# One PSUM bank for all attention outputs, scaled four heads at a time

## The chip, the cores and the metric

One core of one Trainium2 chip runs the whole layer. The metric is the device time of one execution, in microseconds (us), of which three runs of the kernel before gave 663.7, 664.32 and 665.25 us; the median is 664.32 us.

## The reference: what is computed

A decoder layer on 512 tokens of width 1024, in float32: an RMS norm, one input projection, two token mixers side by side (an mLSTM of 4 heads, and a sparse attention of 8 heads of width 64), an output projection, a gated MLP with a short convolution, and a last RMS norm. The change is in the attention. For each block of 128 queries an indexer scores all keys, the best 128 are kept, and the softmax runs over the kept keys only:

```python
logits = einsum('bqhd,bqkhd->bqhk', qa, ks) * (A_DH ** -0.5) + bias      # 8 heads, 4 blocks of 128 queries
p   = softmax(where(valid, logits, -inf), axis=-1)
out = einsum('bqhk,bqkhd->bqhd', p, vs)                                  # 64 outputs for each query and head
```

The kernel doesn't gather: it adds a large negative number to the logits of keys that were not kept, takes the exponentials, multiplies them with all values up to the block's last key, and divides by the row sum at the end. This last step is called the scaling here.

## The kernel before, in words

The order of the instructions on each engine is the order in which the program issues them. A stage has a main list of steps (the matmuls of a projection, in three products of split float32 parts) and side lists; `merge` spreads the side lists over the main list by their costs, at compile time. Each engine then works off its own queue in order and waits where an operand isn't ready.

The attention is the side list `att_steps` (L660 to L755). It has 32 items: item number 8t + h is head h of query block t, t from 0 to 3. It runs as a pipeline. Step i issues, in this order:

- the logits of item i on TensorE (L691, L692 and, for t < 3, L694), into one of three "lg" banks;
- the transposes of item i-3 (L702), copied to SBUF as `pT` by ScalarE (L707) or, for odd heads of block 3, by VectorE (L705);
- for item i-1 the addition of bias and logits with the row minimum on VectorE (L716, called the row reduction below), and the exponential with its row sum on ScalarE (L719);
- in even steps two subtractions on VectorE for later queries (`second`, L680, two instructions a step);
- for block 3 one addition on GpSimd (L727);
- for item i-5 the product of `pT` with the values (L734, called the value product below): t+1 matmuls, into 64 columns of the "av" bank. In the records each of these fp32 matmuls counts twice.

There is one "av" bank of 128x512. In the kernel before, each block takes it anew at head 0 (L731). After head 7 of a block, VectorE takes the reciprocals of the eight row sums (L738, 128x8) and scales the whole bank with one instruction (L741, 128x512). It writes into the place of the block's queries in `aqT`, which were read before. Head 7 of block t falls into step 8t+12, and head 0 of block t+1 into step 8t+13.

The attention runs beside the projections of the mLSTM's inputs (`to_conv` and `to_mv`, L884 to L888). VectorE also has the top-128 search of block 3 there (L533, L536), convolution taps (L778), gate sums (L587 to L591, L610, L612) and the decays of two heads (L815, L819). GpSimd has splits of weights (L125) and casts of queries (L672). The attention outputs are transposed in the next stage (`to_mix`).

Of the kernel before, what the change touches and what calls it, by code (L numbers as in the profile page):

```python
# [10 lines left out]
F32 = mybir.dt.float32  # L11
# [33 lines left out]
def hybrid_layer(ctx: ExitStack, tc: tile.TileContext, a, out):  # L45
    nc = tc.nc
# [5 lines left out]
    small = ctx.enter_context(tc.tile_pool(name="small", bufs=2))  # L52
# [7 lines left out]
    def bank(tag):  # L60
        return ps.tile([128, 512], F32, name="bank_" + tag, tag=tag, bufs={"mm": 2, "lg": 3, "tp": 2, "av": 1}[tag])
# [213 lines left out]
    aqT, av = qv[:, 0:4, :], qv[:, 4:8, :]  # L275
# [173 lines left out]
    def backwards(v):  # L449

        (p, _), (step, n) = v.ap
        return bass.AP(tensor=v.tensor, offset=v.offset + (n - 1) * step, ap=[[p, 128], [-step, n]])
# [199 lines left out]
    ha, rsum, pout = {}, {}, {}  # L652
# [3 lines left out]
    def zeros():  # L656
        nc.gpsimd.tensor_scalar(qlz.rearrange("p a b c -> p (a b) c"), ident[:, None, :].to_broadcast([128, 4, 128]), 0.0,
                                None, op0=OP.mult)

    def att_steps(ts):  # L660
        items = [(t, h) for t in ts for h in range(8)]
        n = len(items)
        lg, ll, lp, qp = {}, {}, {}, {}

        def queries(j):

            t, g = divmod(j, 2)
            qd = ap.tile([128, 2, 2, 128], F32R, name="qd", tag="Q", bufs=2)
            src = aqT[:, 2 * g:2 * g + 2, t * 128:(t + 1) * 128]
            for i, a_, b_ in ((0, slice(0, 64), slice(64, 128)), (1, slice(64, 128), slice(0, 64))):  # L670
                nc.scalar.activation(qd[a_, :, i, :], src[a_], AF.Copy)
                nc.gpsimd.tensor_copy(qd[b_, :, i, :], src[a_])  # L672
            qp[j] = qd

        def second(p):

            t, c = divmod(p, 4)
            src = aqT[:, c, t * 128:(t + 1) * 128]
            for i, a_ in ((0, slice(0, 64)), (1, slice(64, 128))):
                nc.vector.tensor_tensor(qlz[a_, p % 2, i, :], src[a_], qp[p // 2][a_, c % 2, i, :].bitcast(F32), OP.subtract)  # L680

        def step(i):
            if i % 4 == 1 and i // 4 + 1 < n // 4:
                queries(i // 4 + 1)
            if i < n:
                t, h = items[i]
                w = (t + 1) * 128
                lg[i] = bank("lg")
                w2 = max(w, 256)
                qd = qp[i // 4]  # L690
                nc.tensor.matmul(lg[i][:, :w2], qd[:, h // 2 % 2, h % 2, :], kS[:, h, :w2], start=True, stop=False)  # L691
                nc.tensor.matmul(lg[i][:, :w2], qlz[:, i // 2 % 2, h % 2, :], kS[:, h, :w2], start=False, stop=t >= 3)  # L692
                if t < 3:
                    nc.tensor.matmul(lg[i][:, :w2], identb, keep[t] if t else causal[:, None, :].to_broadcast([128, 2, 128]),  # L694
                                     start=False, stop=True)
            if 0 <= i - 3 < n:
                t, h = items[i - 3]
                w = (t + 1) * 128
                l = ll.pop(i - 3)
                pt = bank("tp")  # L700
                for j in range(t + 1):
                    nc.tensor.transpose(pt[:, j * 128:(j + 1) * 128], l[:, j * 128:(j + 1) * 128], ident)  # L702
                pT = ap.tile([128, 512], F32, name="pT", tag="wA", bufs=3)
                if t >= 3 and h % 2:
                    nc.vector.tensor_copy(pT[:, :w], pt[:, :w])  # L705
                else:
                    nc.scalar.activation(pT[:, :w], pt[:, :w], AF.Copy)  # L707
                lp[i - 3] = pT
            if 0 <= i - 1 < n:
                t, h = items[i - 1]  # L710
                w = (t + 1) * 128
                if h == 0:
                    rsum[t] = small.tile([128, 8], F32, name="rs")
                l = ap.tile([128, 512], F32, name="l", tag="wB", bufs=3)
                nm = small.tile([128, 1], F32, name="nm", bufs=4)
                nc.vector.tensor_tensor_reduce(l[:, :w], lg.pop(i - 1)[:, :w],  # L716
                                               backwards(bias["T"][:, h, :w]) if t < 3 else score[t], -1.0, 3.0e38,
                                               OP.add, OP.min, nm)
                nc.scalar.activation(l[:, :w], l[:, :w], AF.Exp, bias=nm, scale=-1.0,  # L719
                                     accum_out=rsum[t][:, h:h + 1])  # L720
                ll[i - 1] = l
            if i and i % 2 == 0 and i // 2 + 1 < n // 2:
                second(i // 2 + 1)
            if i < n and items[i][0] >= 3:

                t, h = items[i]
                nc.gpsimd.tensor_tensor(score[t], backwards(bias["T"][:, h, :(t + 1) * 128]), keep[t], OP.add)  # L727
            if 0 <= i - 5 < n:
                t, h = items[i - 5]
                if h == 0:  # L730
                    pout[t] = bank("av")  # L731
                pT, po = lp.pop(i - 5), pout[t]
                for j in range(t + 1):
                    nc.tensor.matmul(po[:, h * 64:(h + 1) * 64], pT[:, j * 128:(j + 1) * 128],  # L734
                                     av[:, j, h * 64:(h + 1) * 64], start=(j == 0), stop=(j == t))
                if h == 7:
                    rr = small.tile([128, 8], F32, name="rr")
                    nc.vector.reciprocal(rr, rsum[t])  # L738

                    ha[t] = aqT[:, :, t * 128:(t + 1) * 128]  # L740
                    nc.vector.tensor_tensor(ha[t].rearrange("p c (h d) -> p c h d", h=2),  # L741
                                            po.rearrange("p (c h d) -> p c h d", c=4, h=2),
                                            rr.rearrange("p (c h) -> p c h", c=4)[:, :, :, None].to_broadcast([128, 4, 2, 64]),
                                            OP.mult)
        def costed(i):
            def f():
                step(i)
            f.cost = items[min(i, n - 1)][0] + 2.947
            return f
        def ready():  # L750
            zeros()
            queries(0)
            second(0)
            second(1)
        return [ready] + [costed(i) for i in range(n + 5)]  # L755
# [478 lines left out]
```

## Time and profile before

| what | value |
|---|---|
| median of three runs | 664.32 us |
| the profiled execution: its time | 664.08 us |
| its span, first to last instruction | 662.3 us |
| mean granted TensorE clock | 0.992 |
| TensorE matmuls busy | 640.9 us (97%) |
| VectorE busy | 479.4 us (72%) |
| ScalarE busy | 317.7 us (48%) |
| GpSimd busy | 178.3 us (27%) |
| DMA, mean over the span | 142 GB/s |

All times of rows count from the first instruction of the profiled execution. The granted clock is the share of 2.4 GHz that TensorE was given: 1.00 is 2.4 GHz and 0.50 is 1.2 GHz. A time line's row gives the start, the duration, the engine, the line, the operation, the output and the inputs; in brackets stands how long the engine was idle before, and what ended the idle time. Matmuls that follow one another overlap in the records, so a duration is not the cost of one more matmul.

### The profile page before, as it was taken

The numbers are of one execution on the slowest core, as the hardware profiler recorded it, in microseconds if no ns is written. First come the engines' busy times: TensorE is split into PE (matmuls) and PEld (weight loads), VectorE is DVE, ScalarE is ACT, GpSimd is POOL, SyncE is SP. The second block draws the span as 40 slices with busy tenths as digits, with TensorE's granted clock in tenths as the row PEclk, the third lists the DMA queues.
The fourth block names the chain that finished last, engine by engine and source line by source line (L and its number), as shares of the span: only waits on it lengthen the run. The fifth ranks groups of instructions, "written<-read, shape, count | busy, mean of one in ns | idle before, by whom it ended". The sixth has DMA issues, their size and how long they took to land.

```text
span 662.3 us, 9108 instructions
## 1 busy us (share of the span) xinstructions
PE 640.9 (97%) x3386; PEld 546.3 (82%) x3386; DVE 479.4 (72%) x851; ACT 317.7 (48%) x537; POOL 178.3 (27%) x185
## 2 busy tenths in 40 slices
PE   7999999989999999999999999999999999999993
PEld 5977889868889998889988888888888887888882
DVE  4688999979846866756467566666766769998864
ACT  5546355756665624425443343334344345755553
POOL 2132577221452305315021212121221211000043
PEclk9999999989999999999999999999999999999997
DMA  9321443120110311142265557546674565766632
GB/s 304 116 77 64 146 151 105 45 65 1 64 63 3 128 64 63 31 130 89 103 228 158 186 191 254 197 152 223 196 248 170 213 222 182 231 195 201 191 127 96
DMA packets 58028, 93.96 MB, mean 142 GB/s; under 512 B 4643, under 2 KB 41703, under 8 KB 57856
## 3 DMA queue, kind: packets, MB, share of 16 engines
q1 hardware_dynamic: 50464, 65.49, 30.3%
q0 software_dynamic: 6800, 26.32, 11.2%
q10 hardware_dynamic: 720, 1.57, 0.7%
q8 instruction: 27, 0.44, 0.3%
q14 instruction: 17, 0.14, 0.1%
HBM read 79.72 MB, written 13.65 MB: 141 GB/s over the span
## 4 chain that ended last, share of the span: by engine, by line
PE 80%; DVE 10%; issue 3%; ACT 3%; POOL 2%; DMA 1%; ACTq 0%; POOLq 0%; DVEq 0%
PE bank_mm L215 10%; PE bank_mm L217 10%; PE bank_mm L216 10%; PE bank_av L217 5%; PE bank_av L216 5%; PE bank_av L215 5%; DVE score L518 2%; PE bank_mm L386 2%; PE bank_mm L259 2%; PE bank_av L734 2%; PE bank_mm L969 2%; PE bank_mm L971 2%; PE bank_mm L970 2%; PE bank_mm L260 2%; PE bank_mm L261 2%
## 5 line engine op out<-in xcount | busy, mean ns | idle before, releaser
L125 DVE TENSOR_TENSOR wlo<-raw,whi 128x1024 fp32r<-128x1024 f32 x98 | 118.7, 1214 | 55.3 <-ACT whi L124 55.3
L124 ACT ACTIVATE whi<-raw 128x1024 fp32r<-128x1024 f32 x120 | 123.1, 1028 | 72.9 <-PE bank_mm L1127 13.9
L215 PE MATMUL bank_mm<-fh,whi 128*128 128x512 f32 (+1 forms) x248 | 93.2, 376 | 0.0
L217 PE MATMUL bank_mm<-fh,wlo 128*128 128x512 f32 (+1 forms) x248 | 93.1, 375 | 0.0
L216 PE MATMUL bank_mm<-fl,whi 128*128 128x512 f32 (+1 forms) x248 | 93.1, 375 | 0.0
L125 POOL TENSOR_TENSOR wlo<-raw,whi 128x1024 fp32r<-128x1024 f32 x22 | 54.2, 2465 | 72.0 <-ACT whi L124 52.2
L1041 POOL TENSOR_TENSOR y<-yc 128x512 f32<-128x512 f32 x22 | 30.7, 1395 | 141.5 <-DVE yc L1025 141.5
L216 PEld LDWEIGHTS bank_mm<-fl,whi 128*128 128x128 f32 x248 | 46.7, 188 | 8.5
L215 PEld LDWEIGHTS bank_mm<-fh,whi 128*128 128x128 f32 x248 | 46.7, 188 | 8.4
L217 PEld LDWEIGHTS bank_mm<-fh,wlo 128*128 128x128 f32 x248 | 46.7, 188 | 8.4
L215 PE MATMUL bank_av<-fh,whi 128*128 128x512 f32 (+1 forms) x128 | 48.2, 376 | 0.0
L217 PE MATMUL bank_av<-fh,wlo 128*128 128x512 f32 (+1 forms) x128 | 48.1, 376 | 0.0
L216 PE MATMUL bank_av<-fl,whi 128*128 128x512 f32 (+1 forms) x128 | 48.1, 376 | 0.0
L215 PE MATMUL bank_mm<-hh,whi 128*128 128x512 f32 (+1 forms) x112 | 43.9, 392 | 0.0
L217 PE MATMUL bank_mm<-hh,wlo 128*128 128x512 f32 (+1 forms) x112 | 42.5, 380 | 0.0
L1034 ACT ACTIVATE yc<-yc 128x512 f32<-128x512 f32 x22 | 13.9, 632 | 59.0 <-DVE yc L1025 59.0
L216 PE MATMUL bank_mm<-hl,whi 128*128 128x512 f32 (+1 forms) x112 | 42.2, 377 | 0.0
L1159 POOL TENSOR_TENSOR x<-x,gain 128x512 f32<-128x512 f32 x6 | 10.2, 1708 | 90.9 <-ACT xn L1151 90.9
L1084 DVE TENSOR_TENSOR prep<-prep 128x512 f32<-128x512 f32 x44 | 30.1, 685 | 4.2 <-DMA prep<-in_w_down_dram 4.0
L259 PE MATMUL bank_mm<-whi,hh 128*128 128x256 f32 x112 | 32.6, 291 | 0.0
L260 PE MATMUL bank_mm<-whi,hl 128*128 128x256 f32 x112 | 31.6, 282 | 0.0
L261 PE MATMUL bank_mm<-wlo,hh 128*128 128x256 f32 x112 | 31.6, 282 | 0.0
(354 smaller groups left out, 1591.5 us busy)
## 6 DMA issues: line engine op xcount, KB each, us to landing
raw<-in_w_up_dram SPq DMA_DIRECT2D x22, 1024.0 KB, 6.7
raw<-in_w_in_dram SPq DMA_DIRECT2D x13, 1024.0 KB, 5.0
prep<-in_w_down_dram POOLq DMA_DIRECT2D x11, 1024.0 KB, 5.4
tq<-prep POOLq DMA_DIRECT2D x11, 1024.0 KB, 4.6
raw<-tq SPq DMA_DIRECT2D x20, 512.0 KB, 4.4
raw<-in_w_down_dram SPq DMA_DIRECT2D x15, 512.0 KB, 4.5
raw<-in_w_out_dram SPq DMA_DIRECT2D x4, 1024.0 KB
T<-skew POOLq DMA_DIRECT2D x1, 2048.0 KB, 8.6
```

The lines of the kernel that those rows point to most:

```text
L124: nc.scalar.activation(hv, src, AF.Copy)
L125: (eng or nc.vector).tensor_tensor(lv, src, hv.bitcast(F32), OP.subtract)
L215: nc.tensor.matmul(ps_, lh, rh, start=first, stop=False)
L216: nc.tensor.matmul(ps_, lh, rl, start=False, stop=False)
L217: nc.tensor.matmul(ps_, ll, rh, start=False, stop=last)
L259: nc.tensor.matmul(st["ps"], ah, wh[:, i, :], start=(k == 0), stop=False)
L260: nc.tensor.matmul(st["ps"], al, wh[:, i, :], start=False, stop=False)
L261: nc.tensor.matmul(st["ps"], ah, wl[:, i, :], start=False, stop=(k == 7))
L386: nc.tensor.matmul(pz, h_[:, k, sl], w_[:, i, :], start=(p == 0 and k == 0), stop=(p == 2 and k == 7))
L1034: nc.scalar.activation(ys[c][:, 0, :], ys[c][:, 0, :], AF.Silu)
L1041: nc.gpsimd.tensor_tensor(g[:, c, :], y[:, 0, :], y[:, 1, :], OP.mult)
L1084: nc.vector.tensor_tensor(prep[:, o, :], prep[:, x_, :], prep[:, y_, :], OP.subtract)
```

## The change

One tile of the "av" bank is taken once, at the first value product, and kept for all four blocks. The scaling is done after heads 3 and 7, each time for four heads: a reciprocal of 128x4 and a multiplication of 128x256, from one half of the bank into two of the four 128-column groups of the outputs. Head 3 of block t falls into step 8t+8. Everything else is as before.

```diff
-                if h == 0:
-                    pout[t] = bank("av")
-                pT, po = lp.pop(i - 5), pout[t]
+                if not pout:
+                    pout[0] = bank("av")
+                pT, po = lp.pop(i - 5), pout[0]
                 for j in range(t + 1):
                     nc.tensor.matmul(po[:, h * 64:(h + 1) * 64], pT[:, j * 128:(j + 1) * 128],
                                      av[:, j, h * 64:(h + 1) * 64], start=(j == 0), stop=(j == t))
-                if h == 7:
-                    rr = small.tile([128, 8], F32, name="rr")
-                    nc.vector.reciprocal(rr, rsum[t])
+                if h % 4 == 3:
+                    c = h // 4 * 2
+                    rr = small.tile([128, 4], F32, name="rr")
+                    nc.vector.reciprocal(rr, rsum[t][:, h - 3:h + 1])
 
                     ha[t] = aqT[:, :, t * 128:(t + 1) * 128]
-                    nc.vector.tensor_tensor(ha[t].rearrange("p c (h d) -> p c h d", h=2),
-                                            po.rearrange("p (c h d) -> p c h d", c=4, h=2),
-                                            rr.rearrange("p (c h) -> p c h", c=4)[:, :, :, None].to_broadcast([128, 4, 2, 64]),
+                    nc.vector.tensor_tensor(ha[t][:, c:c + 2, :].rearrange("p c (h d) -> p c h d", h=2),
+                                            po[:, c * 128:(c + 2) * 128].rearrange("p (c h d) -> p c h d", c=2, h=2),
+                                            rr.rearrange("p (c h) -> p c h", c=2)[:, :, :, None].to_broadcast([128, 2, 2, 64]),
                                             OP.mult)
```

## Rows read from the trace of the kernel before

**Rows 1.** Busy time by stretch: stretch, its us, each engine's us, granted clock, DMA.

```profile
116.50:206.00 89.50, 85.04 (x567) 73.21 (x566) 69.45 (x185) 54.99 (x131) 30.41 (x31) 0.98 0.13 42
159.00:171.00 12.00, 11.78 (x78) 9.97 (x78) 11.82 (x26) 7.86 (x20) 4.35 (x4) 1.00 0.14 43
206.00:653.00 447.00, 445.51 (x2249) 378.87 (x2248) 312.69 (x461) 201.01 (x295) 95.89 (x104) 1.00 0.49 163
```

**Rows 2.** Waits of TensorE from 116.5 to 206: us, times, longest.

```profile
PE bank_av L734 <- DVE qv L741: 2.6, 2, 2.3
```

**Rows 3.** Time line around the end of block 0.

```profile
135.16 0.36 PE L691 MATMUL bank_lg<-kS,qd 128*128 128x256 f32 x1 [0.60 <-DVE nm L716]
137.38 0.20 DVE L738 RECIPROCAL rr<-rs 128x8 f32<-128x8 f32 x1
137.72 0.69 DVE L741 TENSOR_TENSOR qv<-bank_av,rr 128x512 f32<-128x512 f32 x1
138.32 0.68 DVE L533 MAX8 m<-score 128x8 f32<-128x512 f32 x1
138.46 0.66 PE L734 MATMUL bank_av<-qv,pT 128*128 128x64 f32 x4 [2.26 <-DVE qv L741]
```

**Rows 4.** VectorE by line and shape, 116.5 to 206: count, us, mean ns.

```profile
L716 DVE CUSTOM_DVE_ANT_0 l<-bank_lg,T 128x256 f32<-128x256 f32 x8 | 3.3, 413 | 0.9 <-PE bank_tp L702 0.9
```

**Rows 5.** Time line around heads 3 and 4 of block 0.

```profile
128.06 0.33 PE L734 MATMUL bank_av<-qv,pT 128*128 128x64 f32 x2
128.62 0.75 DVE L778 SCALAR_TENSOR_TENSOR mq<-bank_mm,cw,mq 128x509 f32<-128x509 f32 x1 [0.86 <-ACT mq L775]
128.76 0.33 PE L734 MATMUL bank_av<-qv,pT 128*128 128x64 f32 x2
```

**Rows 6.** Time line around heads 3 and 4 of block 1.

```profile
147.74 0.60 DVE L680 TENSOR_TENSOR ql<-qv,qd 64x128 fp32r<-64x128 f32 x2
148.75 0.56 PE L734 MATMUL bank_av<-qv,pT 128*128 128x64 f32 x4
```

**Rows 7.** Time line to the end of block 1.

```profile
150.26 0.62 ACT L719 ACTIVATE l<-l,nm 128x384 f32<-128x384 f32 x1 [0.58 <-DVE nm L716]
150.87 1.04 ACT L124 ACTIVATE whi<-raw 128x1024 fp32r<-128x1024 f32 x1
152.05 2.41 POOL L125 TENSOR_TENSOR wlo<-raw,whi 128x1024 fp32r<-128x1024 f32 x1 [6.44 <-issue]
151.94 2.67 DVE L680 TENSOR_TENSOR ql<-qv,qd 64x128 fp32r<-64x128 f32 x2
158.47 0.69 DVE L741 TENSOR_TENSOR qv<-bank_av,rr 128x512 f32<-128x512 f32 x1
159.22 0.88 PE L734 MATMUL bank_av<-qv,pT 128*128 128x64 f32 x6 [0.39 <-DVE qv L741]
```

**Rows 8.** Time line around heads 3 and 4 of block 2.

```profile
168.91 1.45 DVE L680 TENSOR_TENSOR ql<-qv,qd 64x128 fp32r<-64x128 f32 x2
169.91 0.78 PE L734 MATMUL bank_av<-qv,pT 128*128 128x64 f32 x6
```

**Rows 9.** Time line from the end of block 2 to the end of block 3.

```profile
179.16 0.18 ACT L620 ACTIVATE em<-bank_tp 128x16 f32<-128x16 f32 x1 [0.79 <-PE bank_tp L619]
195.53 0.67 PE L734 MATMUL bank_av<-qv,pT 128*128 128x64 f32 x5
195.90 0.68 DVE L716 CUSTOM_DVE_ANT_0 l<-bank_lg,score 128x512 f32<-128x512 f32 x1
198.49 1.12 DVE L815 TENSOR_SCALAR sc<-bank_lg,rc 128x128 f32<-128x128 f32 x4 [1.91 <-PE bank_lg L808]
```

**Rows 10.** Busy time by stretch, with the granted clock before DMA's two columns.

```profile
136.20:138.46 2.26, 0.00 (x0) 0.00 (x1) 2.10 (x5) 1.55 (x5) 1.35 (x3) 1.00 0.23 45
139.50:142.95 3.45, 3.45 (x15) 2.98 (x13) 2.45 (x8) 0.90 (x4) 0.00 (x0) 0.51 0.49 169
648.50:650.00 1.50, 0.44 (x2) 0.30 (x2) 0.35 (x1) 1.03 (x3) 0.00 (x0) 1.00 0.58 213
```

## The prediction

> **What bounds the kernel now.** Read the busy time by stretch first. In the attention's stretch, 116.5 to 206 us, TensorE is busy for 85.04 of 89.5 us, and after it for 445.51 of 447 us [rows 1]. A delay of TensorE in the attention is therefore paid in full at the end: behind it there are 1.5 us of idle time in 447. VectorE has 69.45 us of work in the same 89.5, but its share isn't even: from 159 to 171 us it is busy for 11.82 of 12 us, so there nothing that is added to it is made up.
>
> Then read whom TensorE waits for. The longest entry of the stretch is the value product waiting for the scaling: 2.6 us in two waits [rows 2]. The time line shows both. At the end of block 0 the scaling runs from 137.72 to 138.41, and the next block's first value product starts at 138.46, after 2.26 us without work [rows 3]; at the end of block 1 the wait is 0.39 us [rows 7]. These are the waits that the change works on. Their cause is to be seen too: the scaling is late because VectorE reaches it late (2.10 of those 2.26 us it was busy [rows 10]), not because it is long.
>
> **The change part by part.** Two things change: how often TensorE waits for a scaling, and how long a scaling is.
>
> *Whom it concerns.* Before, three value products follow a scaling of the same bank (head 0 of blocks 1, 2, 3). After, seven do, if the half that is filled must wait for the read of the half that is scaled: head 4 of every block comes one step behind the scaling of heads 0 to 3. No row here shows a matmul writing a bank while VectorE reads other columns of it, so this is my choice, with the opposite as a rival below. I choose the wait, because in every case in the trace the first write comes after the end of the whole read, 0.05 us behind it [rows 3, 7].
>
> The Trainium skill ("PSUM — Partial Sum Buffer", section "PSUM bank collisions raise a hardware error") says that TensorE writing and VectorE reading one bank at once is an error even at different columns, and that one must guard by bank, not by address. By that rule the wait at head 4 must be there; a guard by columns alone would leave the rival's sum. No run here shows the collision.
>
> *Price of a half scaling.* From the start of the reciprocal to that of the multiplication it is 0.34 us [rows 3]; a 128x4 reciprocal I take at the same. The multiplication of 128x256 isn't in the trace: half of the present 0.69 is 0.35, and the whole is 0.69. I take 0.41, as a VectorE operation of that shape on a PSUM operand has [rows 4]. VectorE's next instruction begins 0.09 before such a multiplication ends (138.32 against 138.41 [rows 3]), so a half costs VectorE 0.34 + 0.41 - 0.09 = 0.66 us. The scaling at the end of a block becomes 0.28 us shorter.
>
> *Block 0, head 3.* VectorE is idle for 0.86 us before 128.62, so the reciprocal is hidden. The value product of head 3 ends at 128.39, so the multiplication runs from 128.43 to 128.84, head 4 starts at 128.89 instead of 128.76, and VectorE's next work at 128.75 instead of 128.62 [rows 5]. VectorE is late by 0.13. TensorE's own 0.13 disappears in the 2.26 us that it waits later.
>
> *End of block 0.* VectorE is 0.13 later and its scaling 0.28 shorter: -0.15 us for TensorE.
>
> *Block 1, head 3.* The two subtractions before the new instructions end at 148.34 [rows 6]; the half scaling ends at 148.34 + 0.34 + 0.41 = 149.09, and head 4 starts at 149.14 instead of 148.75. TensorE waits 0.39, and VectorE is 0.66 later.
>
> *End of block 1.* Is that 0.66 made up before? The one place is the subtraction that took 2.67 us for two while GpSimd split a weight, from 152.05 to 154.46. But GpSimd waits for ScalarE's copy at 150.87, which stands behind an exponential that waits for VectorE [rows 7], so all of it moves. The scaling ends 0.66 - 0.28 = 0.38 later, which replaces the wait of 0.39 that was there and takes in TensorE's 0.39. Up to here: -0.15 + 0.38 = +0.23 us, for both engines.
>
> *Block 2, head 3.* VectorE is full from 159 to 171, so nothing is made up. The subtractions end at 170.36, because GpSimd works beside them (1.45 us; elsewhere 0.60 [rows 6]). The half scaling ends at 171.11, head 4 starts at 171.16 instead of 169.91 [rows 8]: +1.25 us. Were the subtractions at 0.60, it would be +0.40.
>
> *End of block 2.* The two waits of the stretch [rows 2] are those at the ends of blocks 0 and 1, so there is none here that a shorter scaling could cut: 0.
>
> *Block 3, head 3.* This scaling stands on VectorE behind the decays of a head and the row reduction that runs from 195.90 to 196.58. So it ends at 196.58 + 0.34 + 0.41 = 197.33, and head 4, at 195.53 before, starts at 197.38 [rows 9]: +1.85 us. VectorE itself loses nothing, as it is idle for 1.91 us before 198.49. The work up to here moves with TensorE: ScalarE's activation at 179.16 waits for TensorE, and the exponentials behind it in its queue feed the rest. The last scaling is followed by nothing that TensorE waits for.
>
> *Memory, DMA, steps.* No DMA, no matmul and no step is added, and the order of the side lists is the same. VectorE has 8 instructions more, all counted above; SP's and POOL's queues get none.
>
> Sum: 0.23 + 1.25 + 1.85 = +3.33 us. On the profiled execution's 664.08 us (662.3 of span and 1.8 around it) this gives 667.4; the median of the runs is 0.24 above that execution, so I say 667.5 us. With the ends of the price, the three waits that count change by -0.06 to +0.28 each: -0.2 to +0.8.
>
> *The clock.* After the 2.26 us without work TensorE runs at a granted 0.51 from 139.50 to 142.95, which is the 1.2 GHz level: 3.45 us for about 1.7 us of work [rows 10]. After the idle 1.06 us in 648.5 to 650 the clock stays at 1.00. The new waits of 1.25 and 1.85 us lie between. The 2.26 follows 0.60 us of idle time a microsecond earlier [rows 3], some 2.9 in all, so both new waits, which stand alone, are nearer to the 1.06, and I take no drop; one drop more is +1.7. The wait at the end of block 0 stays above 2 us, so I leave its drop in the sum.
>
> **The rivals.**
>
> *The halves don't wait for each other.* If only equal columns order the two engines, head 4 waits for nothing, and head 0 of the next block only for a scaling four steps older. Then the 2.26 + 0.39 us of waits go, and the clock's drop with them: -2.65 - 1.7 = -4.4. VectorE's additional 0.38 us a block would cost back perhaps 1 us where it is full: 661 us. For it speaks that the two halves share no column; against it, that the trace has no such overlap. This is the case on the other side: faster.
>
> *The delays don't add.* If VectorE's work in block 3 hangs on GpSimd and loaded weights rather than on TensorE, TensorE's earlier lateness is swallowed in the 1.85: then the total is the 1.85 alone, 665.9 on the profiled execution, 666.2 us as a median. If the subtractions of block 2 also lose GpSimd's company, nothing is left of the first waits anyway, and it may end near 665.5. Against it speaks the activation at 179.16 that waits for TensorE.
>
> *One of the new waits drops the clock.* The 1.85 us is the candidate: 667.5 + 1.7 = 669.2 us.
>
> **How the numbers follow.** Two runs of this kernel can't be told apart below about 0.2%, which is 1.3 us. Forecast: 0.50. No wait between the halves: 0.14. The delays don't add: 0.17. One more drop: 0.19. The range: the low end at 664.5 leaves out the first rival and a piece of the second; the high end at 669.8 takes in the drop and half of the price's upper end. Faster by over 0.2% has the first rival's chance without its small tail, 0.13. Within 0.2% (up to 665.6) are that tail and a part of the second rival, 0.12. Slower: 0.75.
>
> **What would show it.** The waits of TensorE for the scaling: five or six instead of two, with the longest still at the end of block 0 and others of 1 to 2 us before head 4 of blocks 2 and 3. Scaling 8 times, about 0.41 us each. TensorE idle for over 6 us in the attention's stretch instead of 4.5. The prediction is wrong if head 4 starts before the half scaling ends, if the multiplication is far from 0.41 us, or if the waits are there and the stretch isn't longer.

## The result, and the profile after

The changed kernel takes 668.9 us (median of five runs, 667.42 to 670.44) against 664.32 before: a ratio of 1.0065, with a 95% interval of 1.005 to 1.008. The profiled execution took 669.08 us, of which 667.4 are the span.

Busy time by stretch after; the columns are those of [rows 1]. The second stretch is as long as the one in [rows 1] and begins 5 us later.

```profile
116.50:211.00 94.50, 87.29 (x567) 74.27 (x566) 70.70 (x193) 54.86 (x131) 30.44 (x31) 0.96 0.12 40
211.00:658.00 447.00, 445.53 (x2249) 378.88 (x2248) 312.41 (x460) 201.12 (x295) 95.98 (x104) 1.00 0.49 163
```

The attention's stretch is 94.5 us long instead of 89.5, for the same 567 records of TensorE. Behind it nothing has changed: 445.53 us busy in 447, against 445.51. So all of the loss arises in the attention, and nothing of it is given back.

The waits of TensorE in that stretch, and the two new kinds of VectorE instruction with count, busy us and mean ns:

```profile
PE bank_av L734 <- DVE qv L743: 5.2, 5, 2.0
PE bank_lg L691 <- DVE nm L716: 1.7, 3, 0.7
```

```profile
L743 DVE TENSOR_TENSOR qv<-bank_av,rr 128x256 f32<-128x256 f32 x8 | 3.4, 425 | 4.6 <-PE bank_av L734 3.9
L740 DVE RECIPROCAL rr<-rs 128x4 f32<-128x4 f32 x8 | 1.4, 175 | 0.1
```

Five waits for the scaling instead of two [rows 2], 5.2 us instead of 2.6. A half scaling takes 425 ns, well over half of the 692 of a whole one. The time line gives each wait its place: the scaling, and the value product behind it.

```profile
128.53 0.42 DVE L743 TENSOR_TENSOR qv<-bank_av,rr 128x256 f32<-128x256 f32 x1 [0.59 <-PE bank_av L734]
129.01 0.43 PE L734 MATMUL bank_av<-qv,pT 128*128 128x64 f32 x2
137.93 0.42 DVE L743 TENSOR_TENSOR qv<-bank_av,rr 128x256 f32<-128x256 f32 x1
138.41 1.03 PE L734 MATMUL bank_av<-qv,pT 128*128 128x64 f32 x4 [1.96 <-DVE qv L743]
...
148.58 0.42 DVE L743 TENSOR_TENSOR qv<-bank_av,rr 128x256 f32<-128x256 f32 x1
149.06 0.66 PE L734 MATMUL bank_av<-qv,pT 128*128 128x64 f32 x4 [0.21 <-DVE qv L743]
159.09 0.42 DVE L743 TENSOR_TENSOR qv<-bank_av,rr 128x256 f32<-128x256 f32 x1
159.57 0.66 PE L734 MATMUL bank_av<-qv,pT 128*128 128x64 f32 x4 [0.32 <-DVE qv L743]
...
169.26 1.46 DVE L680 TENSOR_TENSOR ql<-qv,qd 64x128 fp32r<-64x128 f32 x2
170.73 0.18 DVE L740 RECIPROCAL rr<-rs 128x4 f32<-128x4 f32 x1
171.04 0.42 DVE L743 TENSOR_TENSOR qv<-bank_av,rr 128x256 f32<-128x256 f32 x1
171.52 0.88 PE L734 MATMUL bank_av<-qv,pT 128*128 128x64 f32 x6 [1.10 <-DVE qv L743]
...
197.62 0.68 DVE L716 CUSTOM_DVE_ANT_0 l<-bank_lg,score 128x512 f32<-128x512 f32 x1
198.50 0.42 DVE L743 TENSOR_TENSOR qv<-bank_av,rr 128x256 f32<-128x256 f32 x1
198.98 1.10 PE L734 MATMUL bank_av<-qv,pT 128*128 128x64 f32 x8 [1.56 <-DVE qv L743]
```

In every pair the product starts some 0.05 us after the scaling's end, head 4 as well as head 0. The starts of the value products against those of before, head by head: block 0 head 4 +0.25 us [rows 5]; block 1 head 0 -0.05 [rows 3], head 4 +0.31 [rows 6]; block 2 head 0 +0.35 [rows 7], head 4 +1.61 [rows 8]; block 3 head 4 +3.45 [rows 9]. The decay on VectorE that came at 198.49 [rows 9] comes at 203.50, +5.0. So between head 4 of block 3 and this decay another 1.56 us are lost (that this equals the idle time before head 4 is chance). The granted clock shows to what:

```profile
136.45:138.41 1.96, 0.00 (x0) 0.00 (x0) 1.80 (x5) 1.55 (x5) 1.34 (x3) 1.00 0.13 22
138.54:141.95 3.41, 3.41 (x11) 2.83 (x12) 2.93 (x10) 0.60 (x2) 0.00 (x0) 0.50 0.84 289
197.42:198.98 1.56, 0.00 (x0) 0.00 (x0) 1.40 (x5) 1.56 (x3) 0.50 (x1) 1.00 0.00 0
199.98:203.39 3.41, 3.41 (x14) 2.75 (x14) 0.00 (x0) 0.38 (x1) 0.00 (x0) 0.50 0.00 0
```

Behind the wait at the end of block 0 TensorE runs 3.41 us at the 1.2 GHz level, as before the change [rows 10]. Behind the new wait of block 3 it does so a second time.

### The profile page after: what moved, and what is told of

It is laid out like the page before. It is cut to its first block, busy times and chain, and to the rows that moved or that the text cites. A ratio compares the mean times of both kernels' runs of the same rounds, so it can differ in the third digit from the quotient of the medians.

```text
span 667.4 us, 9124 instructions
## 1 busy us (share of the span) xinstructions
PE 643.0 (96%) x3386; PEld 546.8 (82%) x3386; DVE 480.3 (72%) x859; ACT 317.7 (48%) x537; POOL 178.5 (27%) x185
## 4 chain that ended last, share of the span: by engine, by line
PE 76%; DVE 12%; issue 4%; ACT 3%; POOL 3%; DMA 1%; ACTq 0%; POOLq 0%; DVEq 0%
PE bank_mm L215 10%; PE bank_mm L217 10%; PE bank_mm L216 10%; PE bank_av L216 5%; PE bank_av L217 5%; PE bank_av L215 5%; DVE score L518 2%; PE bank_mm L386 2%; PE bank_mm L972 2%; PE bank_mm L971 2%; PE bank_mm L973 2%; PE bank_mm L259 2%; PE bank_mm L1129 1%; PE bank_mm L1128 1%; PE bank_mm L1130 1%
```

## The experiments

My theory was that of the prediction: head 4 has to wait until the other half of its bank has been read, and each wait lasts as long as the work that VectorE has ahead of the scaling. The rivals were that holding the tile, the number of VectorE instructions, or a late operand costs the time, and that the delays don't add up. Each block of runs was timed beside the kernel before on one chip: 664.09 us in the first block, 664.34 in the second, 663.76 in the third.

**The two parts apart: held, but scaled whole; and scaled in halves, but taken anew.** The first kernel is the kernel before with these lines alone changed:

```diff
-                if h == 0:
-                    pout[t] = bank("av")
-                pT, po = lp.pop(i - 5), pout[t]
+                if not pout:
+                    pout[0] = bank("av")
+                pT, po = lp.pop(i - 5), pout[0]
```

> The bank is held over all four blocks, but scaled eight heads at a time, as in the kernel before. My theory (holding the tile is nothing, since head 0 of the next block waits for the scaling either way): the same time as the kernel before, 664.1 us, with waits of 2.3 and 0.4 us at the ends of blocks 0 and 1. Rival (holding it adds waits): slower by over 1 us.

Measured: 664.12 us against 664.34, ratio 0.9993 (0.9984 to 1.0002), with the same two waits, 2.7 us in all.

The second kernel is the changed one with these three lines put back as they were before.

> The bank is taken anew for each block, as before, but scaled four heads at a time, as in the changed kernel. My theory (the cost is the wait of head 4 for the half scaling of the same bank, and VectorE's lateness): all of the slowdown is here, 667.4 us without and 669 us with a drop of the clock after block 3's wait; four waits at head 4, of about 0.1, 0.2, 1.1 and 1.6 us. Rival (holding one tile over all blocks costs something itself, by waits of later blocks): 664 to 665 us.

Measured: 667.65 us against 664.09, ratio 1.0059 (1.0043 to 1.0076). Five waits, 5.1 us. Head 4 of block 2 is the clearest:

```profile
170.86 0.42 DVE L743 TENSOR_TENSOR qv<-bank_av,rr 128x256 f32<-128x256 f32 x1
171.34 0.88 PE L734 MATMUL bank_av<-qv,pT 128*128 128x64 f32 x6 [1.10 <-DVE qv L743]
```

Holding the tile is worth nothing in either direction. The halves make the whole loss.

**Is it the splitting or the place?** Both half scalings stand after head 7, each with its reciprocal and its multiplication.

```diff
-                if h % 4 == 3:
-                    c = h // 4 * 2
+                if h == 7:
+                    for c in (0, 2):
...
```

> The bank is held, and the two half scalings both stand after head 7. VectorE has the same 16 instructions as in the changed kernel, but head 4 has nothing to wait for. My theory (the place of the half scaling makes the waits): 664.3 + about 1 us = 665.3, as each end of a block gets 0.4 us later and the two waits there grow by that. Rival (the additional VectorE work and fixed costs of splitting are what costs, wherever they stand): 668 to 669 us.

Measured: 664.53 us against 664.09, ratio 1.0007 (0.9998 to 1.0017). The waits at the ends of blocks 0 and 1 are 2.59 and 0.72 us, 0.33 longer each than in [rows 3, 7]. Together that is 0.66 us, where I had expected about 1, and the medians differ by 0.44, with an interval from -0.1 to +1.1.

```profile
138.49 0.66 PE L734 MATMUL bank_av<-qv,pT 128*128 128x64 f32 x4 [2.59 <-DVE qv L741]
159.56 0.88 PE L734 MATMUL bank_av<-qv,pT 128*128 128x64 f32 x6 [0.72 <-DVE qv L741]
```

So the 16 small instructions cost some half a microsecond where the eight stood before; the rest of the change's loss is their place.

**Does the wait come from sharing a bank?** To have a bank for the second half, three kernels have two banks for logits instead of three; the first is the kernel before so changed, the second the changed kernel, and the third differs from the second in one thing alone:

```diff
-                    pout[0] = bank("av")
-                pT, po = lp.pop(i - 5), pout[0]
+                    pout[0], pout[1] = bank("av"), bank("hv")
+                pT, po = lp.pop(i - 5), pout[h // 4]
```

> The kernel before with two banks for logits instead of three; the bank that comes free is unused in the attention. It is the control of the next two. Theory: slower than 664.3, since the logits of an item now wait for the row reduction two items back and VectorE is some 2 us late: 667 to 675 us.

Measured: 678.94 us, ratio 1.0227 (1.0207 to 1.0247), slower than I expected; the logits wait for the row reduction 5.9 us instead of 1.6. Other stages use the same banks, and a part of the loss is theirs: ahead of the attention TensorE waits 5.0 us instead of 1.4 at L501, and behind it 3.5 us at L904, where it did not wait before.

> The changed kernel with two banks for logits. Theory: slower than its control by 1 to 4 us, with value products waiting for the scaling at head 4 and head 0, less than before where the logits already hold TensorE back. Rival: as the control.

Measured: 681.93 us, ratio 1.0269 (1.0254 to 1.0284). Waits of TensorE:

```profile
PE bank_lg L691 <- DVE nm L716: 6.8, 11, 2.4
PE bank_av L734 <- DVE qv L743: 2.1, 4, 1.2
```

> The changed kernel with two banks for logits, and the value products of heads 0 to 3 and 4 to 7 in two banks, each held. Instructions, columns and order are the same as in the kernel with one bank; only which bank the second half lies in differs. My theory (the wait of head 4 comes from sharing the bank with the half that is read, not from columns or from a lack of operands): no value product waits for a scaling at all, and the time is below that of the one-bank kernel by 2 to 5 us. Rival (head 4 waits for something else, such as its transposed exponentials, and the scaling is only named because it ends last): the same idle time before heads 4 and the same time.

Measured: 678.67 us, ratio 1.0234 (1.021 to 1.0258). The waits of TensorE:

```profile
PE bank_lg L691 <- DVE nm L716: 8.1, 12, 2.4
```

Heads 3 and 4 of block 2:

```profile
171.34 0.78 PE L734 MATMUL bank_av<-qv,pT 128*128 128x64 f32 x6
174.19 0.78 PE L734 MATMUL bank_hv<-qv,pT 128*128 128x64 f32 x6
```

No value product waits for a scaling any more. Head 4 of block 2 starts 2.85 us after head 3, as in the kernel before; with one bank it was 3.49, behind a wait of 0.47. The columns that are written and those that are read are disjoint in both kernels; what makes the wait is the common bank. That is the side on which the Trainium skill stands ("PSUM — Partial Sum Buffer", section "PSUM bank collisions raise a hardware error": guard by bank, not by address); the waits of 2.1 us and of none agree with it, as to the order that the program keeps, and no run let the two engines meet in one bank. A tile fills a bank here, so the run doesn't tell apart whether the program keeps the order by the tile or by the bank.

The medians are 3.3 us apart, but the waits are the smaller part of it: the value product's 2.1 us go, and the logits' wait grows by 1.3. The profiled executions are 4.0 us apart, and in the attention TensorE spends 10.24 us at the 1.2 GHz level with one bank (9.50 of them busy) and 3.41 us with two. At half speed that is an estimated 3 us of difference. With one bank, and then with two:

```profile
195.32:205.56 10.24, 9.50 (x41) 8.35 (x40) 2.91 (x9) 2.50 (x6) 3.86 (x4) 0.50 0.31 102
```

```profile
198.10:201.51 3.41, 3.41 (x15) 2.80 (x13) 0.05 (x2) 1.20 (x3) 1.16 (x1) 0.50 0.21 72
```

Against its control (678.94 us) the kernel with two banks wins nothing that is clear of noise. The experiment also shows what the change would have needed, and what that costs here: with the third bank taken from the logits and from the other stages that use it, the whole is 15 us slower than the kernel before.

**Does the order on VectorE set the length of a wait?** In the changed kernel, and in the kernel before, the block of lines with the value product and the scaling is moved ahead of the block with the row reduction. TensorE's order stays the same; VectorE does the scaling before the row reduction and the two subtractions of the step.

```diff
+            if 0 <= i - 5 < n:
+                ...                          # value product and scaling, moved up as they are
             if 0 <= i - 1 < n:
                 t, h = items[i - 1]
...
-            if 0 <= i - 5 < n:
-                ...
```

> The changed kernel with the value product and the scaling issued ahead of the row reduction of their step (TensorE's order stays the same; VectorE does the scaling before the row reduction and the two subtractions). My theory (a wait lasts as long as what VectorE has ahead of the scaling): the 1.1 us of block 2 and the 0.3 of the end of block 1 vanish, the 2.0 of the end of block 0 falls to about 1.1 with no drop of the clock behind it, block 3's falls from 1.6 to about 1.0 to 1.2: 662 to 663.5 us. Rival (the waits come from the sharing of the bank as such, and the order on VectorE is immaterial): 668.9 us.

Measured: 663.57 us against 664.09, ratio 0.999 (0.9981 to 0.9999). The end of block 0 waits 0.18 us, head 4 of block 2 0.20, head 4 of block 3 0.95, and no part of the stretch runs at the lower clock. It is 0.5 us below the kernel before, by the ratios some 5 us below the changed one, and just above the 662 to 663.5 us that I had expected. The wait at the end of block 0 fell further than expected; 1.1 us came anew, as a matmul of the gates (L608) waits for ScalarE, and the logits wait 2.4 us for the row reduction instead of 1.7.

> The kernel before with the same move: value product and whole scaling ahead of the row reduction of their step. My theory: the wait at the end of block 0 falls from 2.26 to about 0.5 us, that at block 1 vanishes, and the clock's drop behind block 0 goes too: -1.8 - 0.4 - 1.7 = -3.9, 660.4 us; 661.5 if VectorE's later row reductions give a part of it back. Rival: no change, 664.3 us.

Measured: 660.7 us against 664.09, ratio 0.9954 (0.9937 to 0.997): faster than the kernel before by 3.4 us, and by the ratios some 7 us faster than the changed one. The end of block 0:

```profile
135.38 0.19 DVE L719 RECIPROCAL rr<-rs 128x8 f32<-128x8 f32 x1
135.71 0.69 DVE L722 TENSOR_TENSOR qv<-bank_av,rr 128x512 f32<-128x512 f32 x1
136.31 0.41 DVE L733 CUSTOM_DVE_ANT_0 l<-bank_lg,T 128x256 f32<-128x256 f32 x1
136.45 0.66 PE L715 MATMUL bank_av<-qv,pT 128*128 128x64 f32 x4 [0.47 <-DVE qv L722]
```

The wait of 2.26 us is 0.47, and the wait at the end of block 1 is gone; the granted clock of the stretch is 1.00. The row reduction now stands behind the scaling, and neither TensorE (1.7 us instead of 1.6) nor ScalarE (18.6 instead of 19.1) waits much longer for it. Of the 3.4 us, an estimated 1.7 are the drop of the clock behind the end of block 0, which this execution doesn't have [rows 10]; the shorter waits are worth 2.2, and a new wait of 0.6 at L608 takes a part back.

**Do the delays add?** The bank is held, and only block 3, or only block 2, is scaled in halves. The kernel for block 3 is shown; the other has `t == 2` in both places.

```diff
-                if h % 4 == 3:
+                if h == 7 or (t == 3 and h == 3):
+                    c, m = (h // 4 * 2, 4) if t == 3 else (0, 8)
...
```

> The bank is held; only block 3 is scaled in two halves, the other blocks with one instruction. My theory (each wait counts in full, and block 3's wait can drop the clock): the wait of head 4 of block 3 is 1.6 us; 665.7 us without a drop of the clock, 667.3 with one. Rival (the delays don't add; block 3's scaling alone, at a fixed time on VectorE, makes the whole loss): 668.9 us, all of the change's loss here, and none for block 2.

Measured: 666.63 us against 664.34, ratio 1.0037 (1.0023 to 1.005). The wait of head 4 of block 3 is 1.56 us:

```profile
196.40 0.42 DVE L742 TENSOR_TENSOR qv<-bank_av,rr 128x256 f32<-128x256 f32 x1
196.88 1.10 PE L734 MATMUL bank_av<-qv,pT 128*128 128x64 f32 x8 [1.56 <-DVE qv L742]
```

```profile
199.00:202.40 3.40, 3.40 (x27) 3.02 (x27) 2.46 (x8) 0.70 (x2) 0.00 (x0) 1.00 0.02 5
```

In this profiled execution (665.59 us) the clock does not drop behind it. The twelve runs go from 665.54 to 669.12 us: five lie below 666, as in this profile, three from 666.6 to 666.8, and four above 667.5.

> The bank is held; only block 2 is scaled in two halves. My theory: the wait of head 4 of block 2 is 0.9 to 1.1 us, with no drop of the clock: 665.2 us. Rival (the delays don't add; the lateness of block 2 is swallowed in block 3, where TensorE waits for work that doesn't move with it): 664.1 us as before.

Measured: 665.56 us, ratio 1.0017 (1.0009 to 1.0026). The wait is 1.10 us, and the clock stays at 1.00 behind it.

```profile
167.20 0.78 PE L734 MATMUL bank_av<-qv,pT 128*128 128x64 f32 x6
171.31 0.88 PE L734 MATMUL bank_av<-qv,pT 128*128 128x64 f32 x6 [1.10 <-DVE qv L742]
```

> The changed kernel again, beside the others on one chip, so that the parts can be added up against it. Theory: 668 to 669 us; the sum of block 3's and block 2's parts and about 0.3 of the first two blocks. Rival (the parts don't add): it stays at the time of block 3's part alone.

Measured: 668.2 us, ratio 1.0061 (1.0046 to 1.0075), +3.9 us. Block 3 alone has +2.3 and block 2 alone +1.2, together 3.5; the 0.4 that is left is near what the first trace of the changed kernel has at head 0 of block 2, +0.35. These are medians of runs with and without drops of the clock; the traces show the same without them. The starts of head 3 of blocks 2 and 3, in the kernel before:

```profile
167.06 0.78 PE L734 MATMUL bank_av<-qv,pT 128*128 128x64 f32 x6
192.78 1.00 PE L734 MATMUL bank_av<-qv,pT 128*128 128x64 f32 x8
```

and in the changed kernel:

```profile
167.41 0.78 PE L734 MATMUL bank_av<-qv,pT 128*128 128x64 f32 x6
194.50 1.00 PE L734 MATMUL bank_av<-qv,pT 128*128 128x64 f32 x8
```

From head 3 to head 4 of block 2 it is 2.85 us before, 4.11 where block 2 alone is split, and 4.11 in the changed kernel. In block 3 it is 2.75 before, 4.49 where block 3 alone is split (head 3 starts at 192.39 there), and 4.48 in the changed kernel. The delays add. In this kernel's profiled execution (667.59 us) the wait at the end of block 0, 1.97 us, is followed by full clock, and the one of block 3 by the lower:

```profile
136.45:138.42 1.97, 0.00 (x1) 0.01 (x1) 1.81 (x5) 1.55 (x5) 1.35 (x3) 1.00 0.14 25
138.42:142.00 3.58, 3.58 (x22) 3.18 (x23) 3.39 (x12) 1.40 (x5) 0.00 (x0) 1.00 0.83 281
198.24:201.65 3.41, 3.41 (x16) 3.14 (x15) 0.00 (x0) 0.22 (x1) 0.00 (x0) 0.50 0.00 0
```

## Why the prediction was right, and where its sizes were off

*Head 4 waits for the half scaling.* Right, and shown: one bank or two for the halves is the difference between waiting and not waiting. The rival of the halves that don't wait for each other falls. All the signs that the prediction named came: five waits, 0.425 us for a half scaling, and 7.2 us of TensorE's idle time in the stretch.

*The price of a half.* 0.41 us expected, 0.425 measured; from the reciprocal's start to the multiplication's it is 0.31 us (170.73 to 171.04) or less instead of 0.34.

*Blocks 0 and 1.* +0.23 us expected up to head 0 of block 2, +0.35 measured. Most of the difference is in block 0, where VectorE gets 0.25 us late instead of 0.13 (128.87 against 128.62). The 0.66 us by which VectorE is late in block 1 isn't made up on the way, as was argued: the two slow subtractions start 0.64 us later and take 2.68 us again, and GpSimd's split beside them also starts 0.64 later.

*Block 2.* +1.25 expected, 1.61 - 0.35 = +1.26 measured. The subtractions lose time beside GpSimd again, 1.46 us.

*Block 3.* +1.85 expected, 3.45 - 1.61 = +1.84 measured between the two heads 4. So close a match is partly luck. Head 3 is already 1.72 us late (194.50 against 192.78), 0.11 more than head 4 of block 2, and that was not in the sum; at head 4 itself 1.73 come on top. The scaling ends 0.62 us after the row reduction (198.30 to 198.92) instead of the 0.75 expected, which makes up for it. The idle time recorded is only 1.56, since matmuls overlap in the records: before, the product began 0.17 us before the end of the transposes ahead of it.

*The sum without the clock.* +3.33 expected, +3.45 measured at head 4 of block 3; block 2 and block 3 alone add up with it. The rival of delays that don't add falls with them. The top of the range, by the prediction's own terms (669.2 and half of 0.8), is 669.6 and not 669.8.

*The clock.* This is the step that missed: "I take no drop". In the profiled execution the wait of block 3 is followed by 3.41 us at the 1.2 GHz level, and the loss between head 4 and the decay behind it is 1.56 us, close to the rival's price of 1.7. The runs split the same way: of the eleven of the changed kernel (five here, six in its second measurement), four at a mean granted clock of 0.992 take 667.29 to 667.70 us, which is the forecast, five at 0.989 or 0.990 take 668.63 to 669.17, which is the rival, and two at 0.987 take over 670. The two profiled executions are of the first kind with one drop in the attention (667.59 us) and of the second with two (669.08). So the forecast is the time of an execution with one drop, and the median of 668.9 has, by its clock, two. It lay inside the range only because the range took in the drop: without it, the price's upper end of +0.8 would have ended at 668.3. Taking the nearest row and its 1.06 us was the mistake: one execution shows one outcome, and a wait of the same length gives the other in the next one. The drop at the end of block 0, which the prediction left in the sum because that wait "stays above 2 us", is no surer: by the prediction's own figures the wait is 2.26 - 0.15 - 0.13 = 1.98 us, it measured 1.96 and 1.97, and one of the two executions has no drop there.

## What to carry to other kernels

Before splitting the read of an accumulator to let writing and reading overlap, see whether the halves lie in one bank: here they did, and the split added waits instead of shortening them. When an engine waits for a short instruction of another, look at what stands ahead of that instruction in its queue: moving the scaling in front of work that was less urgent was worth 3.4 us, about half of it by the clock, and needed no bank. Behind waits of TensorE of 1.56 to 2.26 us the clock fell in some executions here, for some 1.6 us more: count that as a chance and not as yes or no.

## What the runs showed of the hardware that I had not expected

The same wait of TensorE can be followed by the lower clock or not. At the end of block 0, 1.96 us of idle time gave 3.41 us at 0.50 in one execution of the changed kernel, and 1.97 us gave none in another; at block 3, 1.56 us gave 3.41 us at 0.50 in two executions of the changed kernel and none where block 3 alone was split. The kernel before spreads in the same way: of its 29 runs beside the experiments of the second block two took 662.2 and 662.3 us, at a mean granted clock of 0.996, thirteen 663.8 to 664.3 us at 0.992 to 0.994, and fourteen 664.8 to 665.6 us at 0.989 or 0.990. That these steps, and those of the changed kernel, are one drop more or less each is argued from the clock alone; only the profiled executions show where one lies. The mean is a rough guide: it also holds the end of the span, where the clock stands at 0.50 for 4.6 to 7.4 us in the profiled executions with no matmul left (in the kernel before from 654.93 us on), which costs nothing.

Not tried: letting the read of one half and the write of the other half of one bank go on without order. That is a race, so the columns' share in the wait was tested through the banks alone.
